# The opening of a decoder block: request order and row sums of the first modulation, and the gates' columns as one transfer

## The chip, the cores and the metric

The kernel runs on one core of a Trainium2 chip. The metric is the device time of one execution in microseconds (us), the median of several runs. Beside it there is one profiled execution, from which every view in this document is taken. Engines are called as the profile calls them: PE is TensorE (matmuls; PEld its weight loads), DVE is VectorE, ACT is ScalarE, POOL is GpSimd, SP is SyncE, whose queue asks for all data transfers (DMA).

## The reference

One layer of a decoder: a modulation, a mixer with three kinds of heads, and a feed-forward part. Only the beginning matters here. For 2048 positions of width 1024:

```python
c_act = jax.nn.silu(c)                                   # 1024 values
mod = c_act @ w_ada[l] + b_ada[l]                        # 1024 x 6144 weights
sh1, sc1, gt1, sh2, sc2, gt2 = [m[:, None, :] for m in jnp.split(mod, 6, axis=-1)]
h = rms_norm(x, g_mix[l]) * (1.0 + sc1) + sh1
y = hybrid_mixer(h, w_in[l], ...)                        # begins with p = h @ w_in
```

The first thing that the mixer does is the projection `h @ w_in` into 3088 columns. It needs `h`, and `h` needs the first two of the six parts of the modulation: `sh1` (columns 0 to 1023 of `w_ada`) and `sc1` (columns 1024 to 2047). The rest of the kernel (attention, mLSTM, gating, output projection, feed-forward) is not touched by the change.

## The kernel before, in words

All of it is one program without loops at run time. Matmuls are made in three passes over split operands (`mm3`, L53 to L56: high x high, high x low, low x high), each operand having been split into a high part (`hh`, `wh`: a rounded copy) and a low part (`hl`, `wl`: what the rounding left).

The opening, in the order of the program text:

- The vector `c` is loaded as rows, turned on PE (`columns`, L382 to L389) and goes through silu on ACT into `cs` (L398), one column for each of eight row pieces of 128.
- Four tiles of x (128 positions each, 512 KB) are loaded and normalised in place (`norm_x`, L513 to L524): squares on ACT (L518), small steps on DVE, a power on POOL (L128), a scaling on DVE (L523).
- `first_mod(0)` (L437 to L447): for the column groups 0 and 2 of `w_ada` (512 columns each: the first half of `sh1` and of `sc1`) eight pieces of 128 rows x 512 columns, 256 KB each, are loaded into tiles `wa` (L410, buffers of the tag hT, of which there are 32). `mod_sum` (L413 to L421) multiplies each piece by its column of `cs` and adds it to an accumulator, all on DVE: one instruction for the first piece (L418), seven more for the others (L420). PE then sums the accumulator over its 128 rows and turns it into four columns, by four matmuls with a column of ones (L441), into a PSUM tile `modp`. With `g_mix` and `b_ada`, loaded as rows and turned by `columns`, DVE makes `sh1` and `a1` for the first four of the eight 128-column pieces of h (L445 to L447).
- The weights of the first column block, `Weights` (L570 to L597): eight pieces `wr` of 128 x 272, loaded by two transfers each, 256 columns of `k_m` and 16 columns of gates (`load`, L585). `cast` makes `wh` on ACT (L595) and `wl` on POOL (L596).
- `first_mod(1)`, the same for the column groups 1 and 3, for the other four pieces of h.
- `make_h(0)` (L555 to L567): for each of the eight pieces k of width, the four tiles of x are turned on PE into a PSUM tile (L560), ACT scales and shifts it into `h32` with columns k of `a1` and `sh1` (L564), DVE copies it into `hh` (L565) and takes the rest into `hl` (L566).
- `head_setup` (L534 to L550): 13 small loads, of which the last is the spatial weights `wsn` (L541); POOL masks them (L543), PE turns them (L549), ACT copies them into `wT` (L550).
- `make_h(1)`: four more tiles of x (L404), normalised, and the same eight pieces.
- The first block of projections (`natural`, L635): eight row tiles, 24 matmuls of 272 columns each, with three PSUM banks, so that three row tiles can be open at once. Then the second block begins (512 columns a matmul).

Small constants stand in the text between and behind these: the identity as bf16 (L97), a selector `selb` (three casts, L821), causal masks `maskb` and `maskT` (L834, L839), all by DVE, from tiles that POOL fills.

What sets the order: outside the hand-ordered stretches the order of each engine's instructions is made by a planner, when the program is built. It takes of the instructions that are ready, by its own estimate of durations, the one that stands first in the program text. From the second to the sixth block of projections of either half of the positions (`manual_schedule`, entered where i is 1 in the loop over `steps`, the last part of the text below) the order of the text holds; behind them it is the planner's again. In both cases each engine carries out its own list strictly in order, and SP's queue asks for transfers in order. A tile with a tag takes one of that tag's buffers and waits until it is free; the tag tmpA, of which the text below takes several small tiles, has two.

Of the kernel before, what the change touches and what calls it, by code (L numbers as in the profile page):

```python
# [8 lines left out]
F32 = mybir.dt.float32  # L9
# [3 lines left out]
ALU = mybir.AluOpType  # L13
# [4 lines left out]
P = 128  # L18
# [7 lines left out]
KT = D // P  # L26
# [3 lines left out]
C_Q, C_K, C_V, C_QM, C_KM, C_VM, C_US, C_G = 0, 512, 1024, 1536, 1792, 2048, 2560, 3072  # L30
# [3 lines left out]
def trunk(  # L34
# [7 lines left out]
    V, A, G, T = nc.vector, nc.scalar, nc.gpsimd, nc.tensor  # L42
    dma = nc.sync.dma_start
    x, out = x[0], out[0]
    w_ada, w_in, w_out, w_up, w_down = w_ada[0], w_in[0], w_out[0], w_up[0], w_down[0]

    def bc(ap, axis, n):
        u = ap.unsqueeze(axis)
        shape = list(u.shape)
        shape[axis] = n  # L50
        return u.broadcast_to(shape)
# [26 lines left out]
    ident = cst.tile([P, P], F32, name="ident")  # L78
# [5 lines left out]
    ones = cst.tile([P, P], F32, name="ones")  # L84
# [9 lines left out]
    cs = cst.tile([P, KT], F32, name="cs")  # L94
    gq8 = cst.tile([P, 1], F32, name="gq8")
    identb = cst.tile([P, P], BF16, name="identb")
    V.tensor_copy(identb, ident)  # L97
    maskb = cst.tile([P, P], BF16, name="maskb")

    class Mem:  # L100
# [24 lines left out]
    pool, pp = Mem(), Mem(PSUM)  # L125
# [246 lines left out]
    def tr_ps():  # L372
        return pp.tile([P, 512], F32, name="trp", tag="trp")
# [4 lines left out]
    def mps():  # L378
        return pp.tile([P, 512], F32, name="mps", tag="mps")


    def columns(dst, n, *src):  # L382
        r = pool.tile([P, P], F32, name="rows", tag="tmpA")
        o = 0
        for v in src:
            k = v.shape[1] // P
            dma(r[o : o + k], v[0].rearrange("(k p) -> k p", p=P))
            o += k
        return transposed(dst, r, n)  # L389
# [12 lines left out]
    def load_x(tt):  # L402
        xt = pool.tile([P, D], F32, name="xt", tag="t4k")
        dma(xt, x[tt * P : (tt + 1) * P, :])  # L404
        return xt

    def load_ada(col, tag):
        for k in range(KT):
            st = pool.tile([P, 512], F32, name="wa", tag=tag)
            dma(st, w_ada[k * P : k * P + P, col : col + 512])  # L410
            yield st

    def mod_sum(tiles):  # L413

        acc = pool.tile([P, 512], F32, name="modacc", tag="t2k")
        for k, st in enumerate(tiles):
            if k == 0:
                V.tensor_scalar(acc, st, cs[:, 0:1], None, op0=ALU.mult)  # L418
            else:
                V.scalar_tensor_tensor(acc, st, cs[:, k : k + 1], acc, op0=ALU.mult, op1=ALU.add)  # L420
        return acc  # L421

    def rest_of_columns():
        r = pool.tile([P, P], F32, name="rows", tag="tmpA")
        dma(r[0:8], g_ffn[0].rearrange("(k p) -> k p", p=P))
        for i, g in enumerate((g_q, g_k)):
            for j in range(2):
                dma(r[8 + i : 9 + i, 64 * j : 64 * j + 64], g)
        dma(r[10:14], b_s[0])
        dma(r[14:16], g_m_out[0].rearrange("(k p) -> k p", p=P))  # L430
        transposed(colA[:, 24:40], r, 16)
        V.tensor_scalar(gq8, colA[:, 32:33], 0.125, None, op0=ALU.mult)


    modp = mps()

    def first_mod(hf):  # L437
        for n in (hf, 2 + hf):
            acc = mod_sum(load_ada(n * 512, "hT"))
            for j in range(4):  # L440
                T.matmul(modp[:, n * 4 + j : n * 4 + j + 1], acc[:, j * P : (j + 1) * P], ones[:, 0:1], start=True, stop=True)  # L441
        if hf == 0:
            columns(colA[:, 0:24], 24, g_mix, b_ada[:, 0:2048])
        sl, o = slice(hf * 4, hf * 4 + 4), hf * 4
        V.tensor_tensor(sh1[:, sl], modp[:, o : o + 4], ba[:, o : o + 4], op=ALU.add)  # L445
        V.tensor_tensor(a1[:, sl], modp[:, 8 + o : 12 + o], ba[:, 8 + o : 12 + o], op=ALU.add)
        V.scalar_tensor_tensor(a1[:, sl], a1[:, sl], 1.0, gm[:, o : o + 4], op0=ALU.add, op1=ALU.mult)  # L447
# [65 lines left out]
    def norm_x(xin):  # L513
        for xt in xin:
            st = pool.tile([P, 2], F32, name="st", tag="st")
            for q in range(2):
                jk = pool.tile([P, 512], F32, name="jk", tag="sq")
                A.activation(jk, xt[:, q * 512 : q * 512 + 512], AF.Square, accum_out=st[:, q : q + 1])  # L518
            V.tensor_tensor(st[:, 0:1], st[:, 0:1], st[:, 1:2], op=ALU.add)
            st = st[:, 0:1]  # L520
            V.tensor_scalar(st, st, 1.0 / D, EPS, op0=ALU.mult, op1=ALU.add)
            rsqrt(st, 1)
            V.tensor_scalar(xt, xt, st, None, op0=ALU.mult)  # L523
        return xin  # L524

    x0 = norm_x([load_x(i) for i in range(4)])
    first_mod(0)


    wT = pool.tile([P, 4, P], F32, name="wT")  # L530
# [22 lines left out]
    hT = {}  # L553

    def make_h(tb, xin=None):  # L555
        xs = xin if tb == 0 else norm_x(xin or [load_x(tb * 4 + i) for i in range(4)])
        for k in range(KT):
            ps = (tr_ps, acc_ps)[k % 2]() if tb == 0 else tr_ps()
            for i in range(4):
                T.transpose(ps[:, i * P : (i + 1) * P], xs[i][:, k * P : (k + 1) * P], ident)  # L560
            h32 = pool.tile([P, TB], F32, name="h32", tag="t2k")
            hh = pool.tile([P, TB], F32R, name="hh", tag="hT")
            hl = pool.tile([P, TB], F32R, name="hl", tag="hT")
            A.activation(h32, ps, AF.Identity, bias=sh1[:, k : k + 1], scale=a1[:, k : k + 1])  # L564
            V.tensor_copy(hh, h32)  # L565
            V.tensor_tensor(hl, h32, hh.bitcast(F32), op=ALU.subtract)  # L566
            hT[tb, k] = (hh, hl)  # L567


    class Weights:  # L570
# [4 lines left out]
            self.width = sum(w for _, w in parts)  # L575
            self.raw, self.tiles = [], []

        def load(self):
            k = len(self.raw)
            if k == KT:  # L580
                return
            raw = pool.tile([P, 512], F32, name="wr", tag=self.tags[k])
            o = 0
            for col, wd in self.parts:
                dma(raw[:, o : o + wd], w_in[k * P : (k + 1) * P, col : col + wd])  # L585
                o += wd
            self.raw.append(raw[:, : self.width])
# [230 lines left out]
    selb = pool.tile([P, 4, P], BF16, name="selb")  # L818
    V.memset(selb, 0.0)
    for r in (32, 64, 96):  # L820
        V.tensor_copy(selb[r : r + 4], bc(ident[r : r + 4, r : r + 4], 2, P))  # L821
    nebs = [pool.tile([P, 512], BF16, name="neb%d" % i, tag="neb") for i in range(2)]
    for t in nebs:
        V.memset(t, 0.0)
# [6 lines left out]
    m32 = pool.tile([P, P], F32, name="m32", tag="tmpA")  # L831
    G.memset(m32, 0.0)
    G.affine_select(m32, m32, pattern=[[-1, P]], compare_op=ALU.is_ge, fill=NEG, base=0, channel_multiplier=1)
    V.tensor_copy(maskb, m32)  # L834
    maskT = pool.tile([P, 4, P], BF16, name="maskT")
    maskf = pool.tile([P, P], F32, name="maskf", tag="tmpA")
    G.memset(maskf, 0.0)
    G.affine_select(maskf, maskf, pattern=[[1, P]], compare_op=ALU.is_ge, fill=NEG, base=0, channel_multiplier=-1)
    V.tensor_copy(maskT, bc(maskf, 1, 4))  # L839
    V.memset(rmask, 1.0)  # L840
    V.memset(rmask.rearrange("p (n l) -> p n l", l=P)[:, :, 0:1], 0.0)

# [82 lines left out]
    def mlstm(qi):  # L925
# [32 lines left out]
        def turned(n):  # L958
# [7 lines left out]
            got["k", n] = kT  # L966

        load(0)
        load(1)
        yield  # L970
# [98 lines left out]
    chores.append(rest_of_mod())  # L1069
    written = ExitStack()  # L1070
    cur = Weights(blocks[0][0], G, ("q2k",) * 3 + ("qhl",) * 3 + ("wr",) * 2)
    for k in range(KT):
        cur.load()
    for k in range(KT):
        cur.cast()
    first_mod(1)
    for n, (half, i) in enumerate(steps):
        if i == 0:
            make_h(half * 2, x0)
            if half == 0:  # L1080
                head_setup()
            make_h(half * 2 + 1)
        elif n == nb - 1:
            x0 = [load_x(8 + t) for t in range(4)]
# [21 lines left out]
        cur = nxt[0]  # L1106
# [51 lines left out]
    hT = {}  # L1158
# [587 lines left out]
```

## Time and profile before

| | us |
|---|---|
| median of 3 runs | 2605.19 |
| lowest, highest | 2605.05, 2606.72 |
| the profiled execution, its own time | 2607.8 |
| span of its profile | 2606.1 |

| engine | busy us | share of the span |
|---|---|---|
| PE | 2530.5 | 97% |
| DVE | 2010.0 | 77% |
| ACT | 1272.8 | 49% |
| POOL | 402.5 | 15% |

How to read the views. A line of the timeline begins with the start in us and the length of a merged run of equal instructions in us; then come engine, line of the kernel, operation, output <- input by the program's names with their shapes, and the count; in brackets, how long the engine was idle before it and what released it. A line of a group has the busy time, the mean duration of one in ns and the idle time before. In a table by windows each engine has its busy time and, in brackets, its number of instructions. The chain of waits goes from instruction to instruction back to whatever released it; its lines are start, length and what it was. Durations of matmuls include a part that overlaps with the next; the pitch from start to start is shorter.

### The profile page before, as it was taken

To read this page: it belongs to the slowest core of one execution; us is meant where nothing else is said; L and a number is where in the kernel's file an instruction comes from. 1 tells how busy PE (TensorE), PEld (TensorE's weight loads), DVE (VectorE), ACT (ScalarE), POOL (GpSimd) and SP (SyncE) were. 2 spreads that over 40 slices of the span, in tenths; PEclk is the share of its full clock that TensorE was granted. 3 is DMA by queue.
4 is the path that set the end of the run, shared out by engine and by line. 5 is a ranking of instruction groups with operands and counts; after the bars stand their busy time and mean duration, and the time that the engine had idled before them with its cause. 6 is when DMAs were issued, how large, how long until landed. Compare 5 with 4: busy or idle time off the path is not lost.

```text
span 2606.1 us, 36311 instructions
## 1 busy us (share of the span) xinstructions
PE 2530.5 (97%) x12521; PEld 2097.9 (81%) x12537; DVE 2010.0 (77%) x3438; ACT 1272.8 (49%) x2424; POOL 402.5 (15%) x532
## 2 busy tenths in 40 slices
PE   5999999999999999999989999999999999999999
PEld 5888888888787877777868888888888888888787
DVE  7657666476388889866589888888888887997797
ACT  4333343432388878844455544454444444444443
POOL 2012310132266556520000000000000000000000
PEclk9999999999999999999999999999999999999999
DMA  7345763454664445266632222255222217658523
GB/s 247 107 120 160 209 209 88 129 152 138 180 164 123 129 126 166 58 195 224 248 89 92 79 89 82 81 201 187 90 81 81 90 65 279 210 176 290 184 93 117
DMA packets 302592, 379.58 MB, mean 146 GB/s; under 512 B 31934, under 2 KB 194588, under 8 KB 300360
## 3 DMA queue, kind: packets, MB, share of 16 engines
q1 hardware_dynamic: 302408, 377.26, 46.1%
q8 instruction: 99, 1.62, 0.3%
q14 instruction: 85, 0.70, 0.1%
HBM read 276.44 MB, written 100.74 MB: 145 GB/s over the span
## 4 chain that ended last, share of the span: by engine, by line
PE 81%; DVE 9%; DMA 4%; ACT 3%; issue 2%; POOL 1%; SPq 0%; DVEq 0%; ACTq 0%; POOLq 0%
PE ub L56 11%; PE ub L54 11%; PE ub L55 11%; PE acc L54 6%; PE acc L56 6%; PE acc L55 6%; PE db L55 4%; PE db L56 4%; PE db L54 4%; PE sp L206 3%; PE tp L259 3%; PE op L245 2%; PE op L246 2%; PE wps L55 2%; PE wps L54 2%
## 5 line engine op out<-in xcount | busy, mean ns | idle before, releaser
L54 PE MATMUL acc<-wh,hh 128*128 128x512 f32 (+2 forms) x768 | 285.5, 373 | 1.9 <-DVE vhl L762 1.2
L54 PE MATMUL ub<-T,wsph 128*128 128x512 f32 x704 | 274.2, 390 | 5.8 <-ACT wsph L1358 5.8
L56 PE MATMUL ub<-T,wspl 128*128 128x512 f32 x704 | 273.7, 389 | 1.6 <-DVE wspl L1359 1.6
L56 PE MATMUL acc<-wh,hl 128*128 128x512 f32 (+2 forms) x768 | 274.2, 360 | 0.3 <-DVE hl L566 0.3
L55 PE MATMUL acc<-wl,hh 128*128 128x512 f32 (+2 forms) x768 | 273.9, 358 | 0.2
L55 PE MATMUL ub<-T,wsph 128*128 128x512 f32 x704 | 273.9, 389 | 0.0
L55 PE MATMUL db<-wspl,wsph 128*128 128x512 f32 x616 | 240.6, 391 | 3.6 <-DVE wspl L1490 3.5
L56 PE MATMUL db<-wsph,wspl 128*128 128x512 f32 x616 | 239.6, 389 | 0.0
L54 PE MATMUL db<-wsph 128*128 128x512 f32 x616 | 238.3, 389 | 0.3 <-ACT wsph L1489 0.3
L1358 ACT CAST wsph<-S 128x512 fp32r<-128x512 f32 x176 | 109.7, 623 | 228.4 <-PE ub L55 162.8
L263 DVE TENSOR_TENSOR plo<-tp,phi 128x512 fp32r<-128x512 f32 (+1 forms) x320 | 187.0, 607 | 31.6 <-ACT phi L262 29.4
L54 PE MATMUL ub<-B,wsph 128*128 128x512 f32 x528 | 207.1, 392 | 2.8 <-ACT wsph L1358 2.8
L56 PE MATMUL ub<-B,wspl 128*128 128x512 f32 x528 | 207.2, 392 | 0.6 <-DVE wspl L1359 0.6
L55 PE MATMUL ub<-B,wsph 128*128 128x512 f32 x528 | 207.0, 392 | 0.0
L223 ACT ACTIVATE L<-L,nm 128x1024 f32<-128x1024 f32 (+2 forms) x192 | 172.6, 903 | 36.0 <-DVE nm L212 34.7
L262 ACT CAST phi<-tp 128x512 fp32r<-128x512 f32 (+1 forms) x320 | 160.0, 521 | 40.2 <-PE tp L259 38.9
L259 PE MATMUL tp<-ident,L 128*128 128x128 f32 x1088 | 177.0, 274 | 2.5 <-POOL L L228 0.6
L206 PE MATMUL sp<-kk,q 128*128 128x512 f32 (+3 forms) x640 | 169.2, 375 | 3.3 <-DVE nm L212 2.2
L1489 ACT CAST wsph<-act 128x512 fp32r<-128x512 f32 x132 | 82.3, 623 | 179.0 <-PE db L55 162.2
L228 POOL TENSOR_SCALAR L<-L,rs 128x1024 f32<-128x1024 f32 (+2 forms) x192 | 167.2, 881 | 11.0
L56 PEld LDWEIGHTS acc<-wh,hl 128*128 128x128 f32 x768 | 145.0, 190 | 22.3 <-DVE hl L566 0.8
L54 PEld LDWEIGHTS acc<-wh,hh 128*128 128x128 f32 x768 | 146.2, 191 | 20.7 <-DVE vhl L762 1.4
(333 smaller groups left out, 5942.9 us busy)
## 6 DMA issues: line engine op xcount, KB each, us to landing
w<-in_w_up_dram SPq DMA_DIRECT2D x88, 512.0 KB
wd<-in_w_down_dram SPq DMA_DIRECT2D x176, 256.0 KB
wa<-in_w_ada_dram SPq DMA_DIRECT2D x96, 256.0 KB
act_d<-yc SPq DMA_DIRECT2D x44, 512.0 KB
act<-act_d SPq DMA_DIRECT2D x44, 512.0 KB
wr<-in_w_in_dram SPq DMA_DIRECT2D x64, 256.0 KB
q<-q_d SPq DMA_DIRECT2D x128, 128.0 KB
hc_d<-hl SPq DMA_DIRECT2D x28, 512.0 KB
```

Source lines behind the costliest of these rows:

```text
L54: T.matmul(ps, lh, rh, start=start, stop=False, skip_group_check=resume)
L55: T.matmul(ps, lh, rl, start=False, stop=False, skip_group_check=resume)
L56: T.matmul(ps, ll, rh, start=False, stop=stop, skip_group_check=resume)
L206: T.matmul(sp[:, b : b + bw], q2[n][:, qs], kk[:, s0 + b : s0 + b + bw], start=n == 0, stop=n == 1 and not last)
L223: A.activation(L[c], L[c], AF.Exp, bias=nm[:, n - 1 : n], scale=-1.0, accum_out=rs[:, c : c + 1])
L228: G.tensor_scalar(t, t, rs[:, 0:1], 1.0, op0=ALU.mult, op1=ALU.mult)
L245: T.matmul(op[:, c0:], vv[:, j, :], hi[:, c0:], start=(j == 0), stop=False)
L259: T.transpose(tp[:, i * P : (i + 1) * P], rows[i][j // 8][:, (j % 8) * P : (j % 8 + 1) * P], ident)
L262: A.copy(hi[:, c0:], tp[:, c0:])
L263: V.tensor_tensor(lo[:, c0:], tp[:, c0:], hi[:, c0:].bitcast(F32), op=ALU.subtract)
L1358: A.copy(hi, src)
L1489: A.copy(hi, v)
```

## The change

It has these parts:

- `first_load` requests all 16 pieces of one half at once. The second half's (`first_load(1)`) stand in the text directly behind `first_mod(0)` and so ahead of the column weights, where they stood behind them.
- In each sum of eight pieces, pieces 0, 2, 4 and 6 stay on DVE. Pieces 1, 3, 5 and 7 are multiplied and summed by PE: four matmuls a piece, with the piece as weights and its column of `cs` as the one moving column, added into the four columns of `modp`. The accumulator's four matmuls add into the same columns. `modp` is set to zero first, and no matmul clears it.
- The 16 gates' columns of all eight pieces of the first column block come in one transfer into a tile `gw` (tag tmpA), and POOL copies them piece by piece into `wr`; the eight transfers of 256 columns stay.
- The copies `hh` of the first row block move from DVE to ACT.
- Six casts of constants (`identb`, three of `selb`, `maskb`, `maskT`) move from DVE to POOL.

```diff
-    V.tensor_copy(identb, ident)
+    G.tensor_copy(identb, ident)
...
     modp = mps()
-
-    def first_mod(hf):
+    V.memset(modp[:, 0:16], 0.0)
+
+    def first_load(hf):
+        return {n: list(load_ada(n * 512, "hT")) for n in (hf, 2 + hf)}
+
+    def first_mod(hf, tiles):
         for n in (hf, 2 + hf):
-            acc = mod_sum(load_ada(n * 512, "hT"))
-            for j in range(4):
-                T.matmul(modp[:, n * 4 + j : n * 4 + j + 1], acc[:, j * P : (j + 1) * P], ones[:, 0:1], start=True, stop=True)
+            acc = pool.tile([P, 512], F32, name="modacc", tag="t2k")
+
+            def add(w, col):
+                for j in range(4):
+                    T.matmul(
+                        modp[:, n * 4 + j : n * 4 + j + 1], w[:, j * P : (j + 1) * P], col,
+                        start=False, stop=True, skip_group_check=True,
+                    )
+
+            for k, st in enumerate(tiles[n]):
+                if k == 0:
+                    V.tensor_scalar(acc, st, cs[:, 0:1], None, op0=ALU.mult)
+                elif k % 2 == 0:
+                    V.scalar_tensor_tensor(acc, st, cs[:, k : k + 1], acc, op0=ALU.mult, op1=ALU.add)
+                else:
+                    add(st, cs[:, k : k + 1])
+            add(acc, ones[:, 0:1])
...
     x0 = norm_x([load_x(i) for i in range(4)])
-    first_mod(0)
+    ada = first_load(0)
+    first_mod(0, ada)
+    ada = first_load(1)
...
-            V.tensor_copy(hh, h32)
+            if tb == 0:
+                A.copy(hh, h32)
+            else:
+                V.tensor_copy(hh, h32)
...
-        def load(self):
+        def load(self, n=2):
...
-            for col, wd in self.parts:
+            for col, wd in self.parts[:n]:
...
-        V.tensor_copy(selb[r : r + 4], bc(ident[r : r + 4, r : r + 4], 2, P))
+        G.tensor_copy(selb[r : r + 4], bc(ident[r : r + 4, r : r + 4], 2, P))
...
-    V.tensor_copy(maskb, m32)
+    G.tensor_copy(maskb, m32)
...
-    V.tensor_copy(maskT, bc(maskf, 1, 4))
+    G.tensor_copy(maskT, bc(maskf, 1, 4))
...
     cur = Weights(blocks[0][0], G, ("q2k",) * 3 + ("qhl",) * 3 + ("wr",) * 2)
+    gw = pool.tile([P, KT, 16], F32, name="gw", tag="tmpA")
+    dma(gw, w_in[:, C_G : C_G + 16].rearrange("(k p) n -> p k n", p=P))
     for k in range(KT):
-        cur.load()
+        cur.load(1)
+        G.tensor_copy(cur.raw[k][:, 256:272], gw[:, k, :])
     for k in range(KT):
         cur.cast()
-    first_mod(1)
+    first_mod(1, ada)
```

More of the change, by code (lines that the diff above doesn't have):

```diff
@@ L411, in load_ada @@
             yield st
[L413 to L421, printed above, removed]
     def rest_of_columns():
```

## The prediction, on record before the result

> **What bounds the kernel now.** I read the page's slices first, then the windows by stage.
>
> ```profile
> span 2606.1 us, 36311 instructions
> PE   5999999999999999999989999999999999999999
> ```
> ```profile
> 0.00:47.28 47.28, 19.09 (x75) 15.73 (x75) 36.70 (x81) 14.55 (x32) 14.60 (x28) 1.00 0.82 275
> 47.28:53.50 6.22, 6.22 (x29) 6.13 (x29) 4.84 (x11) 3.00 (x6) 0.07 (x1) 1.00 0.59 231
> 53.50:78.28 24.78, 24.70 (x194) 23.88 (x193) 17.71 (x43) 16.98 (x40) 2.21 (x4) 1.00 0.42 123
> 78.28:2606.10 2527.82, 2480.47 (x12228) 2052.19 (x12242) 1950.74 (x3305) 1238.23 (x2349) 385.65 (x500) 1.00 0.46 143
> ```
> ```profile
> 78.28 0.39 PE L54 MATMUL acc<-hh,wh 128*128 128x512 f32 x1
> ```
>
> Columns after the window's length: busy us (count) of PE, PEld, DVE, ACT, POOL, then clock, DMA share, GB/s. PE is the bound from 47.28 us on; only ahead of that does it idle, 28 of 47 us. At 78.28 us the second weight block (the first in hand-written order) begins, and PE is busy for 98% of what follows. So a change to the start is worth what it moves 78.28; the rest follows unchanged. The chain of waits says what fills the start:
>
> ```profile
> 2.60 6.42 DMA xt<-in_x_dram
> ...
> 14.44 5.50 DMA wa<-in_w_ada_dram
> ...
> 21.28 2.27 DMA wr<-in_w_in_dram
> ...
> 43.97 1.88 PE mps L441 x8
> ```
> ```profile
> 31.15 5.48 DVE L420 SCALAR_TENSOR_TENSOR modacc<-wa,cs,modacc 128x512 f32<-128x512 f32 x7
> 36.54 0.48 DVE L418 TENSOR_SCALAR modacc<-wa,cs 128x512 f32<-128x512 f32 x1
> 37.06 2.33 DVE L420 SCALAR_TENSOR_TENSOR modacc<-wa,cs,modacc 128x512 f32<-128x512 f32 x3
> 39.30 0.42 DVE L565 CAST hh<-h 128x512 fp32r<-128x512 f32 x1
> ...
> 51.49 0.69 DVE L566 TENSOR_TENSOR hl<-h,hh 128x512 fp32r<-128x512 f32 x1
> ```
>
> Arrivals bound it to 19.9 us (14.44 + 5.50). Then DVE does: the second half's sums run on to 44 us, the first copy of h gets its turn among them at 39.3 only, and the last hl of the first row block is ready at 52.2.
>
> **The change, part by part.**
>
> *Sums.* These groups are of the first 47.28 us (count | busy us, mean ns | idle before).
>
> ```profile
> L420 DVE SCALAR_TENSOR_TENSOR modacc<-wa,cs,modacc 128x512 f32<-128x512 f32 x28 | 21.6, 780 | 0.5
> L441 PE MATMUL mps<-ones,modacc 128*128 128x1 f32 x32 | 7.5, 355 | 16.0 <-DVE modacc L420 16.0
> ```
>
> DVE loses 16 of the 28 additions, 16 x 0.78 = 12.5 us. TensorE gains 16 pieces x 4 = 64 matmuls; eight such took 1.88 us in the chain, so 0.235 each, 15.0 us, inside its 28 idle us. A piece costs TensorE 0.94 us and DVE 0.78; a pair comes every 1.3 us or more (below), so both keep up and arrival becomes the bound. (The Trainium skill, "TensorE: Matmul & The Clock Gate", section "LDWEIGHTS (loading the stationary operand)", gives a weight load as columns over 1.2 GHz, 107 ns for 128: a piece would cost 0.43 us, an estimate from that page, and the last sums would end 1.0 us sooner. The trace's 0.235 us per pair does not agree, and I use the trace.) The memset of the sums' bank lies in the idle start: nothing.
>
> *Order of the requests.*
>
> ```profile
> 14.40:20.00 5.60, 1.33 (x5) 0.93 (x5) 5.34 (x10) 0.00 (x0) 1.05 (x3) 1.00 1.01 354
> 20.00:25.00 5.00, 2.09 (x9) 1.96 (x9) 4.75 (x9) 2.09 (x5) 1.67 (x4) 1.00 0.61 137
> 30.00:35.00 5.00, 0.00 (x0) 0.00 (x0) 4.82 (x7) 1.45 (x2) 0.83 (x2) 1.00 1.02 362
> ```
> ```profile
> wa<-in_w_ada_dram SPq DMA_DIRECT2D x96, 256.0 KB
> ```
>
> The second sixteen pieces, 4.19 MB at 362 GB/s, take 11.6 us behind the first: from 19.9 to about 31. The column weights (eight pieces of 128 x 272 floats, 1.11 MB) come behind them. Between 20 and 25 us such traffic moved 137 GB/s at a share of 0.61, so 225 GB/s when busy: 4.9 us, first piece near 32, last near 36. Before, they were there by 27 and waited; that cover is gone.
>
> *Second sums.* Last piece 31, its four matmuls and the accumulator's four 1.9 us, then 1.1 to the first h that needs them (43.97 + 1.88 to 46.98 in the next rows): 34.0, where it was 47.0. The 32 pieces fill the 32 buffers that h's copies use as well; each is free once its sum has read it, all by 34.
>
> *ACT and POOL.*
>
> ```profile
> L1358 ACT CAST wsph<-S 128x512 fp32r<-128x512 f32 x176 | 109.7, 623 | 228.4 <-PE ub L55 162.8
> ```
> ```profile
> 23.99 6.84 POOL L596 TENSOR_TENSOR wl<-wr,wh 128x272 fp32r<-128x272 f32 x8
> ```
> ```profile
> 46.98 0.78 ACT L564 ACTIVATE h<-trp,sh,a 128x512 f32<-128x512 f32 x1 [5.13 <-DVE a L447]
> 52.98 0.59 ACT L550 COPY wT<-mp 128x512 f32<-128x512 f32 x1 [3.21 <-PE mp L549]
> 53.46 0.64 ACT L518 ACTIVATE jk<-xt 128x512 f32<-128x512 f32 x1
> ```
> ```profile
> 8.90 0.78 POOL L128 TENSOR_TENSOR st<-st,nhalf 128x1 f32<-128x1 f32 x1 [0.92 <-DVE st L521]
> ...
> 14.54 0.20 POOL L832 MEMSET m<- 128x128 f32 x1
> ```
>
> ACT takes 8 copies of h, by L1358 0.62 us each; DVE loses them. From 34.0, four h and copies (0.78 + 0.62) with at most eight weight casts of 0.42 (estimate: L1358 scaled to 272 columns, rounded up) between them last to 43.0; the last hl is ready near 43.7, against 52.2. The casts now wait for the column weights and for POOL's copy of the gates' columns, and h stands behind them on ACT. If the planner puts all eight ahead of every h, the eight pairs (11.2 us) run from 36.4 to 47.6, the last hl comes at 48.3: still 4 us ahead. POOL gets eight copies of the gates' 16 columns, not in this trace: between 0.20 (the memset, larger and without an input) and 0.78 (128x1 with two inputs). I take 0.20, since a copy has one input and no power. With 6.84 / 8 = 0.86 for each wl: 33.5 + 8 x 1.06 = 42; at the upper end 46.6. The gates' tile takes one of two small buffers that the masks use, which POOL, idle then, frees in time. Neither end is later than TensorE needs them, since at the rate of 47.28 to 53.50 (6.22 / 29 = 0.21 us) three row tiles use a piece of nine matmuls in 1.9 us. The other casts moved to POOL (six, none larger than 512 columns, 0.9 us each at wl's rate at most if scaled up to 512) stand in its idle time before 23 us (1.1 busy of 5.6 us in the window from 14.40): nothing; without that cover they would stand ahead of wl, 5 us.
>
> So the first projections start near 34 instead of 47.28.
>
> *The second row block is late next.*
>
> ```profile
> 16.47 8.64 SPq L585 DMA_DIRECT2D wr<-in_w_in_dram  x16
> 25.16 9.75 SPq L410 DMA_DIRECT2D wa<-in_w_ada_dram  x16
> ...
> 41.79 0.38 SPq L541 DMA_DIRECT2D wsn<-in_w_s_dram  x1
> 42.21 2.14 SPq L404 DMA_DIRECT2D xt<-in_x_dram  x4
> ```
> ```profile
> SPq L410 <- DMA wa<-in_w_ada_dram: 5.2, 14, 0.9
> ```
> ```profile
> 3.07 11.70 SPq L410 DMA_DIRECT2D wa<-in_w_ada_dram  x16
> ```
> ```profile
> 45.56 1.79 POOL L543 TENSOR_SCALAR_AFFINE_SELECT wsn<-wsn 128x128 f32<-128x128 f32 x4 [14.73 <-DMA wsn<-in_w_s_dram]
> ```
> ```profile
> 51.89 1.05 PE L549 MATMUL mp<-ident,wsn 128*128 128x128 f32 x4
> ```
> ```profile
> 71.73 0.69 DVE L566 TENSOR_TENSOR hl<-h,hh 128x512 fp32r<-128x512 f32 x1
> ```
>
> SP's queue issues one transfer after another up to x at 42.21, and holds back issues until earlier pieces have landed. The change takes out seven issues (16 to 9) of 8.64 / 16 = 0.54 us: 3.8 us. But the second wa may now go at the pace of the first (11.70 instead of 9.75), 1.9 us back. So wsn and x are asked for 1.9 to 3.8 us earlier; I take 2.9. From wsn hangs ACT's chain: masked on POOL 3.8 us after its issue (42.7, when wl is done), ready 44.5; turned on TensorE, where before it stood 4.5 us in the queue (47.35 to 51.89); then wT, then the squares of x, 1.6 us after the turning. The queue's delay can be anything from 0 to 4.5; I take 2, as TensorE is ahead now: squares at 48.1 instead of 53.46. From there to 78.28 were 24.8 us, of which 5.9 lie behind the last hl (72.4); the work then left is 24 + 9 matmuls at 24.78 / 194 = 0.128, 4.2 us, so 1.6 us can go. Second block at 48.1 + 24.8 - 1.6 = 71.3: **7.0 us earlier**. Ends: all of the 3.8 with no queue delay, with the mask done at 43.7, 68.5 (-9.8); only 1.9 with 4.5, 74.8 (-3.5).
>
> The profiled execution took 2607.8 us, span 2606.1; it would become 2600.8. It lies 2.6 above the median of the runs, 2605.19; from that, 2598.2.
>
> **Rivals.** *First: TensorE alone sets it* (the turning and x's squares are not late). 223 instructions ran from 47.28 to 78.28 and nine projections before: starting at 34, 29 in 6.2 us, 203 at 0.128: 66.2, 12 us earlier, 2593.1. For it: x can come by 48; against: ACT's in-order wait for wT. The windows show 0.21 us per instruction up to 53.50 and 0.128 after, at a granted clock of 1.00 in both. (The same page, section "Part 1: The HAM clock gate (the "warmup" mystery)", says that TensorE runs at half rate until a window of about 3.4 us was busy. By that the sums on TensorE could bring full speed before 34 and save 29 x 0.09 = 2.5 us more of this rival, which is 2590.6. The step in the rows agrees; no row shows whether one-column matmuls count as busy.)
>
> *Second: the lead is lost* at wsn and x: the planner, which orders this stage by its own clock, puts the turning behind all four row tiles, or leaves the column weights' requests where they were. Then x's 1.9 to 3.8 us of SP time is all that is won: 0 to 3.5 us earlier, about 2603.
>
> *Third, slower: the gates' one transfer.* All eight casts now wait for it.
>
> ```profile
> DMA packets 2905, 2.14 MB, mean 203 GB/s; under 512 B 1368, under 2 KB 2416, under 8 KB 2904
> q1 hardware_dynamic: 2904, 2.13, 74.7%
> ```
>
> These are the packets of 16.5 to 27 us: 16 engines x 10.5 us x 0.747 = 125 us of engine time. At 362 GB/s the 488 of 2 KB take 44 and the 1048 of 1 KB 47, so a small one costs 0.025 us. The transfer is 1024 rows of 64 bytes; spread over 16 engines 1.6 us, on one 26 us: asked for near 27.5 it lands at 54, the projections start 8 us later than now, 2613. It decides from where it lands after 45.5, 18 us, fewer than two engines. Against: wsn, also regrouped with partitions outermost, was there 3.8 us after its issue.
>
> **How the numbers follow.** Forecast 0.55, first rival 0.20, second 0.17, third 0.08. A difference of 0.2%, 5.2 us, is about what a measurement of this kernel tells from none. The forecast's own range is 2595.4 to 2601.7, of which some three quarters lie beyond 5.2 us: faster 0.40 + 0.20 = 0.60; within 0.2% 0.15 + 0.17 = 0.32; slower 0.08. The range runs from the first rival's 2593 less 0.5 to the middle of the second and a little beyond, 2592.5 to 2604.
>
> **What would show it.** Right: sums of the second half end near 33 us; casts of wr from 32 us; first projection near 34; SP's x near 39; squares at 45 to 51; the first 128x512 projection of the second block near 71; the stretch behind it 2528 us as before. Wrong: gates' columns landing after 45; wsn's turning still at 50 or later; PE idle over 5 us between the row blocks; a longer stretch after the second block's start.

## The result and the profile after

The change made the kernel slower. The median went from 2606.01 us (2605.05 to 2613.88, 6 runs) to 2622.83 us (2617.54 to 2625.55, 6 runs): ratio 1.0055, 95% interval 1.0041 to 1.0069. The profiled execution after was the quickest of its six, 2617.54 us with a span of 2615.8.

First the windows of the kernel after, cut at its own stages (length; busy us and count of PE, PEld, DVE, ACT, POOL; granted clock, DMA share, GB/s), and the second block's first projection:

```profile
0.00:51.92 51.92, 41.23 (x194) 40.63 (x195) 20.53 (x52) 13.61 (x29) 13.62 (x32) 1.00 0.79 278
51.92:60.00 8.08, 7.11 (x28) 6.17 (x29) 3.17 (x7) 6.76 (x14) 5.74 (x7) 1.00 0.01 3
60.00:68.00 8.00, 8.00 (x64) 7.83 (x64) 1.88 (x10) 3.68 (x11) 1.52 (x5) 1.00 0.34 98
68.00:72.00 4.00, 2.44 (x19) 1.90 (x17) 2.60 (x8) 4.00 (x13) 1.11 (x2) 1.00 0.36 101
72.00:76.00 4.00, 2.11 (x9) 1.48 (x10) 3.17 (x8) 1.90 (x4) 0.55 (x1) 0.68 0.25 70
76.00:80.00 4.00, 4.00 (x20) 4.00 (x20) 3.97 (x9) 2.46 (x5) 0.00 (x0) 0.50 0.55 159
80.00:92.31 12.31, 12.31 (x99) 12.31 (x98) 7.30 (x16) 5.94 (x11) 0.00 (x0) 0.99 0.25 77
92.31:2615.80 2523.49, 2477.14 (x12244) 2050.68 (x12242) 1950.50 (x3305) 1238.01 (x2349) 386.13 (x500) 1.00 0.46 143
```
```profile
92.31 0.40 PE L54 MATMUL acc<-hh,wh 128*128 128x512 f32 x1
```

The second block starts at 92.31 us instead of 78.28, 14.0 later. The span grew by only 9.7, because the stretch behind was 4.3 shorter in this execution; the medians stand 16.8 apart. Runs of one and the same kernel are up to 11 us apart (before: 2601.75 to 2612.68 on the chip of the last four experiments), so the stretch behind, known from one execution of each kernel, explains nothing here, and the start of the second block is the better gauge. For the changed kernel and the twelve experiments below, the change of the median and the change of that start agree within 3 us.

The 14.0 us have two parts. PE's row sums come first (timeline, PE):

```profile
12.20 1.71 PE L437 MATMUL mps<-cs,wa 128*128 128x1 f32 x8
...
32.60 6.99 PE L437 MATMUL mps<-cs,wa 128*128 128x1 f32 x32 [0.54 <-DVE a L454]
39.44 1.85 PE L437 MATMUL mps<-ones,modacc 128*128 128x1 f32 x8
41.40 1.71 PE L437 MATMUL mps<-cs,wa 128*128 128x1 f32 x8
45.13 1.71 PE L437 MATMUL mps<-cs,wa 128*128 128x1 f32 x8
46.94 3.41 PE L437 MATMUL mps<-cs,wa 128*128 128x1 f32 x16
50.22 1.84 PE L437 MATMUL mps<-ones,modacc 128*128 128x1 f32 x8
51.92 0.57 PE L54 MATMUL acc<-wh,hh 128*128 128x272 f32 x1
```
```profile
L437 PE MATMUL mps<-cs,wa 128*128 128x1 f32 x128 | 27.6, 346 | 0.5 <-DVE a L454 0.5
L446 DVE SCALAR_TENSOR_TENSOR modacc<-wa,cs,modacc 128x512 f32<-128x512 f32 x12 | 9.3, 771 | 0.6 <-DMA wa<-in_w_ada_dram 0.3
```

The last two lines are groups of the first 52 us. Four matmuls are written for a piece, and the trace has **eight** records for it: 128 for the 16 pieces, and 128 loads of weights beside them (PEld). An f32 matmul is two loads of weights and two passes here. A piece takes 1.71 us, 16 of them 27.4. The second half's sums end at 52.06 (50.22 + 1.84), where DVE alone ended them at 45.84.

Then the second row block (timeline; ACT, then PE, then DVE, then SP's queue):

```profile
53.10 0.78 ACT L574 ACTIVATE h<-trp,sh,a 128x512 f32<-128x512 f32 x1 [7.48 <-DVE a L455]
...
64.97 0.59 ACT L560 COPY wT<-mp 128x512 f32<-128x512 f32 x1 [1.17 <-PE mp L559]
65.45 0.63 ACT L526 ACTIVATE jk<-xt 128x512 f32<-128x512 f32 x1
```
```profile
64.33 0.60 PE L559 MATMUL mp<-ident,wsn 128*128 128x128 f32 x4
```
```profile
67.83 0.75 DVE L531 TENSOR_SCALAR xt<-xt,st 128x1024 f32<-128x1024 f32 x1 [0.53 <-POOL st L128]
...
72.86 0.75 DVE L531 TENSOR_SCALAR xt<-xt,st 128x1024 f32<-128x1024 f32 x1 [0.66 <-POOL st L128]
```
```profile
26.29 0.38 SPq L1086 DMA_DIRECT2D gw<-in_w_in_dram  x1
26.88 6.29 SPq L598 DMA_DIRECT2D wr<-in_w_in_dram  x8
...
38.21 8.01 SPq L404 DMA_DIRECT2D xt<-in_x_dram  x4
```

x is asked for at 38.21, 4.0 earlier than before, and yet its squares begin at 65.45, 12.0 later: on ACT they stand behind wT, wT waits for the turning on PE at 64.33, and in PE's list some 60 projections of the first block stand ahead of the turning, by its records, where 27 did before. From the squares to the second block it takes 26.9 us instead of 24.8. In this stretch PE runs dry: 2.44 and 2.11 busy of 4 us each between 68 and 76. The granted clock falls to 0.68 and 0.50, and in the four busy microseconds from 76 to 80 there are 20 instructions instead of the 32 of full speed. So 12.0 us are lost ahead of the squares and 2.0 behind them.

### The profile page after: what moved, and what is told of

It is laid out like the page before. It is cut to its first block, busy times and chain, and to the rows that moved or that the text cites. A ratio compares the mean times of both kernels' runs of the same rounds, so it can differ in the third digit from the quotient of the medians.

```text
span 2615.8 us, 36565 instructions
## 1 busy us (share of the span) xinstructions
PE 2554.4 (98%) x12665; PEld 2125.0 (81%) x12665; DVE 1993.1 (76%) x3409; ACT 1276.4 (49%) x2432; POOL 408.7 (16%) x546
## 4 chain that ended last, share of the span: by engine, by line
PE 44%; DVE 5%; DMA 1%; issue 0%; ACT 0%; SPq 0%; DVEq 0%; ACTq 0%
PE ub L56 11%; PE ub L54 10%; PE ub L55 10%; PE db L55 4%; PE db L56 4%; PE db L54 4%; DVE wspl L1506 2%; DMA wd<-in_w_down_dram 1%; PE wps L54 0%; PE wps L56 0%; PE wps L55 0%; DVE T L1201 0%; DVE t2w L1491 0%; DVE t2w L1486 0%; DMA ld<-yt_d 0%
```

## The experiments

Each kernel was measured in three rounds. In the table "sums" is the end of the last accumulator's matmuls, "squares" the first squares of the second row block on ACT, "block 2" the first 128x512 projection, all from each kernel's profile. Ratios are to the kernel before on the same chip, whose medians were 2608.74 (beside e1 to e5), 2608.22 (e6 to e8 and e10) and 2607.34 us (the others).

| kernel | sums | squares | block 2 | median us | ratio (95%) |
|---|---|---|---|---|---|
| before | 45.84 | 53.46 | 78.28 | 2606.01 | |
| after | 52.06 | 65.45 | 92.31 | 2622.83 | 1.0055 (1.0041 to 1.0069) |
| e1 all sums on DVE | 44.07 | 56.72 | 82.54 | 2612.17 | 1.0014 (1.0005 to 1.0024) |
| e2 before, sums on PE | 51.22 | 59.85 | 84.62 | 2616.83 | 1.0029 (1.0018 to 1.0041) |
| e4 order of requests back | 52.56 | 61.19 | 86.20 | 2616.05 | 1.0028 (1.0015 to 1.0040) |
| e5 half of the matmuls | 38.53 | 51.98 | 78.77 | 2606.93 | 0.9994 (0.9984 to 1.0004) |
| e6 head later | 52.16 | 59.34 | 89.33 | 2619.70 | 1.0044 (1.0028 to 1.0061) |
| e7 one piece in eight, head later | 39.77 | 47.18 | 77.17 | 2609.22 | 1.0001 (0.9991 to 1.0010) |
| e8 before, head later | 44.92 | 41.45 | 77.79 | 2610.48 | 1.0010 (1.0001 to 1.0020) |
| e9 half of the matmuls, head later | 38.68 | 45.86 | 75.06 | 2604.41 | 0.9989 (0.9978 to 1.0000) |
| e10 all on DVE, head later | 43.93 | 49.97 | 79.00 | 2608.94 | 1.0003 (0.9993 to 1.0013) |
| e11 e7 with four copies back | 40.37 | 46.21 | 77.12 | 2606.12 | 0.9992 (0.9983 to 1.0001) |
| e12 e11 with two in eight | 40.56 | 45.85 | 77.77 | 2604.43 | 0.9982 (0.9973 to 0.9992) |
| e13 copies back on DVE | 52.15 | 69.11 | 95.42 | 2625.59 | 1.0062 (1.0045 to 1.0079) |

The theory (A): the row sums on TensorE cost nearly twice what the prediction gave them, and all of the start hangs from their end. The rivals: B, the order of the requests; C, the casts and copies that now stand in order on ACT.

**All sums back on DVE (e1).**

```diff
-                elif k % 2 == 0:
+                elif True:
```

> The changed kernel with all eight pieces of each sum on VectorE again; request order, gates' transfer, copies on ScalarE and casts on GpSimd stay changed. Theory A (TensorE's row sums cost twice what was forecast: each f32 matmul is two loads and two matmuls, 1.71 us a piece, 34.8 us in all, and in order they hold up the turning of x and the first projections): the second half's sums end on VectorE near 39 us, the second block starts near 70 to 74 instead of 92, time 2596 to 2602. Rival B (the request order and the gates' transfer make the start late): the second block still starts after 85, time above 2614. Rival C (the eight copies on ScalarE and the work on GpSimd make it late): like B.

Measured: block 2 at 82.54, ratio 1.0014. 9.8 of the 14.0 us come back, so the sums on TensorE are the larger part. But it is still 4.3 later than before, though its sums end 1.8 earlier: A missed (it had the sums end near 39 and block 2 start at 70 to 74), and something else is at work.

**The sums on TensorE alone, in the kernel before (e2).**

```diff
+    V.memset(modp[:, 0:16], 0.0)
...
-            acc = mod_sum(load_ada(n * 512, "hT"))
...
+            for k, st in enumerate(load_ada(n * 512, "hT")):
...
+                elif k % 2 == 0:
+                    V.scalar_tensor_tensor(acc, st, cs[:, k : k + 1], acc, op0=ALU.mult, op1=ALU.add)
+                else:
+                    add(st, cs[:, k : k + 1])
+            add(acc, ones[:, 0:1])
```

> The kernel before with the odd pieces' sums on TensorE and nothing else. Theory A: TensorE has 34.8 us of sums in order, the second half's end near 50 us; second block at 85 to 95, time 2613 to 2624. Rivals B and C: no slower than before, 2600 to 2607.

Measured: 84.62 and 1.0029. The median, 2616.83, lies in A's range, and block 2 0.4 us ahead of its. With the old order of requests, the old copies and the old gates the row sums alone cost 6.3 us of the start.

**The order of the requests back (e4):** the column weights are asked for ahead of the second sixteen pieces again, the rest as changed.

```diff
-    ada = first_load(1)
...
     for k in range(KT):
         cur.cast()
+    ada = first_load(1)
     first_mod(1, ada)
```

> The changed kernel with the second half's sixteen pieces requested behind the column weights again, the rest as changed. Theory A: TensorE's sums still set it, 2614 to 2625. Rival B: back to 2608 or less.

Measured: 86.20 and 1.0028. The median lies in A's range, so the order alone is not the cause, as B had it. But with sums as late as these, it adds 6.1 us. The sums end at 52.56 with the old order and at 52.06 with the new one, so the earlier arrival of the pieces buys 0.5 us, and the column weights behind them come later. With the old order all eight wl were done at 28.07 us and wsn was masked at 42.80, ahead of the end of the sums; with the new one POOL makes six of the wl from 54.26 on and masks wsn behind them, at 59.49. One window from 40 us to the second block, e4 first, then after, shows it in POOL: e4 has 4.6 us of work left there, after 10.5, as the wl come so late.

```profile
40.00:86.20 46.20, 44.36 (x289) 42.72 (x289) 24.18 (x57) 26.15 (x54) 4.58 (x8) 1.00 0.39 123
```
```profile
40.00:92.31 52.31, 47.90 (x288) 45.60 (x288) 24.65 (x57) 29.00 (x62) 10.53 (x17) 0.93 0.34 107
```

PE has the same work in both, 289 and 288 instructions. With the new order it is idle for 4.4 us of the window instead of 1.8, and it is busy 3.5 us longer over that work, at a granted clock of 0.93 instead of 1.00. So the dry stretch between the row blocks and the falling clock come largely with the order of the requests. From before over e2 and e4 to after, the 14.0 us are 6.3 for the sums, 1.6 for the gates' transfer, the copies and the casts together, and 6.1 for the order; taken in another sequence, the shares may differ.

**Half of the matmuls of each odd piece (e5)** takes away half of the suspected cost and leaves the order of the text as it is.

```diff
-            def add(w, col):
-                for j in range(4):
+            def add(w, col, cols=4):
+                for j in range(cols):
...
-                    add(st, cs[:, k : k + 1])
+                    add(st, cs[:, k : k + 1], 2)
```

> The changed kernel with two of the four matmuls of each odd piece left out, so that half of the columns lack the odd pieces: a piece then costs TensorE 0.86 us, what the prediction had reckoned. Theory A: the sums end near 37 us, the second block starts at 70 to 76, time 2596 to 2604. Rivals B and C: within 3 us of the changed kernel.

Measured: the sums end at 38.53, 13.5 earlier; block 2 starts at 78.77, 13.5 earlier. Their end passes through to the second block one for one, so it is shown that the length of the sums sets that start in the changed kernel; B and C, which had allowed 3 us, are out as its only cause. A's own ranges (70 to 76, 2596 to 2604) are missed: at 38.53 the sums end 7.3 us ahead of before, and the second block starts no earlier than before. Its windows show where the lead goes:

```profile
52.00:56.00 4.00, 3.68 (x30) 3.46 (x29) 1.43 (x6) 4.00 (x15) 1.10 (x2) 1.00 0.65 189
56.00:60.00 4.00, 1.73 (x12) 1.17 (x11) 2.56 (x7) 2.61 (x8) 1.10 (x3) 1.00 0.29 95
60.00:64.00 4.00, 3.15 (x14) 2.75 (x15) 3.87 (x9) 2.73 (x4) 0.00 (x0) 0.51 0.46 130
64.00:68.00 4.00, 4.00 (x24) 4.00 (x24) 3.67 (x8) 2.84 (x4) 0.00 (x0) 0.64 0.42 110
```

PE finishes the first row block and has nothing of the second: 3.4 of 12 us are dry, then the clock falls to 0.51 and 0.64. The second theory (D): the second row block's x is late, since the turning of wsn and its wT stand ahead of the squares.

**The head's loads and the turning behind the second row block,** in the changed kernel (e6), in the kernel before (e8), with all sums on DVE (e10), and with one piece in eight on TensorE (e7; `elif k != 7` for `elif k % 2 == 0`):

```diff
             make_h(half * 2, x0)
+            make_h(half * 2 + 1)
             if half == 0:
                 head_setup()
-            make_h(half * 2 + 1)
```

> The changed kernel with the thirteen small loads, the masking, the turning and wT placed behind the second row block's make_h in the text. Theory D (beside A: ScalarE's in-order wT waits for a turning that the planner put behind two row tiles, so that the second row block comes late, TensorE runs dry between the row blocks and its clock falls to half): the squares of x follow the first block's h at once, no dry stretch, no granted clock under 1.00 before the second block; the second block starts at 83 to 87 instead of 92, 2 to 8 us less than the changed kernel, still slower than before because of the sums. Without D: within 2 us of the changed kernel and the clock still falls.

> The kernel before with the small loads behind the second make_h alone. In it TensorE was busy throughout between the row blocks, so D expects little: second block at 76 to 78.5, within 3 us of before.

> All sums on VectorE as in the first experiment, the small loads behind the second make_h. D: the second block starts at 73 to 77 instead of 82.5, the clock stays at 1.00, time 5 to 9 us below the first experiment. Without D: as the first experiment.

> The changed kernel with only the last of eight pieces of each sum on TensorE (four pieces of 32 in all) and the small loads behind the second make_h. A and D together: TensorE's sums 14 us instead of 35, no dry stretch; second block at 68 to 74, time 4 to 9 us below before. If a further cause is at work: second block at 77 or later, no better than before.

Measured: in e6 the squares come 6.1 us earlier and block 2 only 3.0 (89.33). D had 83 to 87 and no falling clock, but PE still runs dry and its clock still falls:

```profile
64.00:68.00 4.00, 2.96 (x23) 2.47 (x21) 2.60 (x8) 1.79 (x7) 1.86 (x4) 1.00 0.57 164
68.00:72.00 4.00, 3.13 (x16) 2.52 (x17) 2.97 (x11) 3.00 (x4) 0.68 (x3) 0.74 0.86 246
```

In e8 the first squares come 12.0 earlier, between the fourth and the fifth h, and block 2 only 0.5, as was expected: in the kernel before, moving the turning wins next to nothing. (PE ran dry there for 1.5 us between 40 and 44, and its granted clock reads 0.54 and 0.60 in the two windows from 44 to 52, so the run does not say what the turning alone is worth.) e10 stands 3.5 us ahead of e1 and its clock does not fall; 5.5 to 9.5 were expected. In e7 the sums end at 39.77 and block 2 starts at 77.17, 1.1 ahead of before, against an expected 4 to 10, which is the reading for a further cause: the lead of 6 us in the sums is lost again between the row blocks. Moving the turning helps with the new order of requests, and is a part of the second cause, not all of it.

The table holds a rival to D, the order of the requests. From the end of the sums to block 2 it takes 32.4 to 33.6 us in the four kernels with the old order (before, e2, e4, e8), although the turning was moved in e8 alone, and 35.1 to 43.3 in all the others. The turning would then be one link of what the late column weights hold up: casts, wl, the mask of wsn, the turning. No kernel has short sums on TensorE and the old order together, so how much of the lead of e5 and e7 the order takes is not shown.

**Both suspected causes taken away (e9):** half of the matmuls, and the head later.

> The changed kernel with two of the four matmuls of each odd row piece left out (so half of the columns of sh1 and a1 lack these pieces) and the head's loads and the turning of wsn behind the second make_h, so that both suspected causes are taken away at once. Theory F, two causes in a row (the length of the row sums on TensorE, then the lateness of the second row block because ACT works its list in order and the turning of wsn stands ahead of the squares of x): squares of x at 46 to 48.5 us instead of 51.98, TensorE is dry for under 2 us between the row blocks instead of 3, second block at 73 to 75.5 instead of 78.77, time 2600 to 2604. Rival G, the second block follows the end of the sums alone (about 40 us behind the first projection at 38.4): second block at 78 to 79, 2605 to 2609.

Measured: block 2 at 75.06, as F expected; the squares, at 45.86, lie 0.1 ahead of its range and the median of 2604.41 0.4 above it. G's ranges are missed. PE loses 1.9 us between the row blocks and the clock stays at 1.00:

```profile
52.00:56.00 4.00, 2.38 (x18) 1.88 (x17) 2.19 (x7) 1.35 (x3) 2.11 (x6) 1.00 0.87 255
56.00:60.00 4.00, 3.75 (x29) 3.01 (x28) 3.97 (x11) 3.79 (x7) 0.00 (x0) 1.00 0.59 175
```

The two edits give 17.3 of the start together, 13.5 and 3.7 more. They show also what there was to win with the odd pieces at half their price and the turning out of the way, in the new order of requests: 3.2 us of the start, a ratio of 0.9989 whose interval touches 1.

**The copies of h.** All eight back on DVE in the changed kernel (e13), and the last four back in e7 (e11: `if tb == 0 and k < 4`).

> The changed kernel with nothing but the eight copies hh of the first row block back on DVE: what this part alone is worth. Theory F: the sums on TensorE still end at 52 and the turning of wsn at 64 still gates the squares of x, so ACT is 5 us freer behind 52 to little use: second block at 89.5 to 92.5 instead of 92.31, 2616 to 2623. Rival: the copies on ACT, in order ahead of casts and squares, are the main loss: second block at 85 to 88, 2610 to 2615.

> The changed kernel with one row piece in eight on TensorE, the head's loads behind the second make_h, and of the eight copies hh of the first row block the last four on DVE again, where they were before. Theory F: ACT, the engine on which h, the copies, the casts and the squares of x stand in order, has 4 x 0.62 = 2.5 us less ahead of the squares: squares at 44.5 to 45.5 instead of 47.18, second block at 74 to 75.5 instead of 77.17, 2604 to 2607 where the kernel without this edit took 2609.2. Rival G: second block at 76.5 to 78, 2607.5 to 2611.

Measured: e13 starts block 2 at 95.42, 3.1 later than after, and both F (89.5 to 92.5) and its rival (85 to 88) are missed, as they are in the median. So the copies on ACT helped the start, and C falls as far as they go; the casts are taken up below. In time the two kernels can't be told apart (1.0062 and 1.0055, with intervals that overlap). In e11 block 2 hardly moved (77.12). The fifth h waits for a1 until 41.95 whoever makes the copies, so the squares come 1.0 earlier and not 2.5, and the last four of them stand on ACT behind a copy of the first results, which waits for PE:

```profile
41.95 0.78 ACT L574 ACTIVATE h<-trp,sh,a 128x512 f32<-128x512 f32 x1 [2.64 <-DVE a L455]
...
48.57 0.20 ACT L526 ACTIVATION_READ_ACCUMULATOR jk<-xt 128x1 f32 x1
50.96 0.37 ACT L674 COPY ev<-acc 128x256 f32<-128x256 f32 x1 [2.19 <-PE acc L56]
51.23 0.63 ACT L526 ACTIVATE jk<-xt 128x512 f32<-128x512 f32 x1
```

By the start of block 2 G was right: the planner put another wait of the same kind in the place of the one removed. The median, 2606.12, lies in F's range and 1.4 below G's.

**Two pieces in eight on TensorE (e12),** else as e11: `elif k % 4 != 3`.

> As the one with four copies back, but two row pieces in eight on TensorE. If DVE's sums set their end there (28 additions of 0.78 us with the first pieces' hl among them), four fewer end them 2 to 3 us earlier, near 38 instead of 40.6, and the second block starts at 72 to 74, 2602 to 2606. If TensorE's pieces of 1.71 us set it, the sums end no earlier or later (40.5 to 43) and the second block starts at 75 to 78, 2607 to 2611.

Measured: the sums end at 40.56, as in e11, block 2 at 77.77. At their end PE's rows follow each other without a gap, so TensorE's price sets it, by the second reading:

```profile
35.33 1.71 PE L437 MATMUL mps<-cs,wa 128*128 128x1 f32 x8
36.90 0.45 PE L570 MATMUL trp<-ident,xt 128*128 128x128 f32 x1
37.14 1.71 PE L437 MATMUL mps<-cs,wa 128*128 128x1 f32 x8
38.71 1.85 PE L437 MATMUL mps<-ones,modacc 128*128 128x1 f32 x8
```

The time, 2604.43, is below that reading's range and lies in the other's. This is the best version: 0.9982 (0.9973 to 0.9992), the only one whose interval lies below 1. But only 0.5 us of its 4.7 (0.18% of 2607.34; the two medians are 2.9 apart) show at the second block; where the rest comes from stays open, and its interval overlaps that of e11.

## Why the prediction was wrong, step by step

**The bound: right.** PE is busy for 98% of what follows the second block's start, and the time went where that start went: 14.0 us later, 16.8 in the medians.

**The sums: the step that failed.** "Eight such took 1.88 us in the chain, so 0.235 each, 15.0 us": the eight were taken for eight written matmuls, and they were the four of one accumulator. The row quoted for it had the means to see this: "L441 ... x32" in the first 47 us, where the program text writes 4 matmuls for each of 4 accumulators, 16. So a piece costs TensorE 1.71 us and not 0.94, the sixteen 27.4 and not 15.0, and "both keep up and arrival becomes the bound" turns round: DVE's part, 0.77 a piece, is done early, and PE falls behind by almost a microsecond a piece. The sums ended at 52.06 instead of about 33, and the first h that needs them came at 53.10 instead of 34.0. What DVE loses was right: 12 additions, 9.3 us, remain of 28.

The step had a second fault: it set the 15.0 us against the 28 idle us of the whole start, and asked only whether a piece keeps up with a piece. In the stretch in which the pieces arrive, PE also has the accumulators' matmuls and the turning of x. In e5, with the odd pieces at 0.85 us, PE was busy for 25.9 of the 26.5 us from 12 to 38.53, 20.6 of them with the sums. So about at the forecast's price, too, TensorE and not arrival sets the end of the sums, 5.5 us later than forecast.

(The Trainium skill's 107 ns a load, which the prediction set against its 0.235, is half of what a record took here, 27.4 / 128 = 0.214, and there are twice as many records as it was applied to. By the section on the clock gate of the same page of the Trainium skill, "TensorE: Matmul & The Clock Gate", a cold TensorE runs at half rate, and that would account for the first factor.) The timeline of e7 agrees: the same group of eight records takes 1.86 us early and 1.03 after PE has turned x.

```profile
27.34 1.86 PE L437 MATMUL mps<-cs,wa 128*128 128x1 f32 x8 [0.54 <-DVE a L454]
...
36.55 0.63 PE L570 MATMUL acc<-ident,xt 128*128 128x128 f32 x2
36.97 1.03 PE L437 MATMUL mps<-cs,wa 128*128 128x1 f32 x8
```

At that pace a piece costs close to the forecast's 0.94; in the changed kernel none of the sixteen ran at it.

**The order of the requests: right in its times, a cost in effect.** x was asked for at 38.21 (forecast 39). The prediction saw that the column weights lose their cover and reckoned that this costs nothing; e4 shows the price once the sums are late, 6.1 us.

**The gates' one transfer: not the cause.** The third rival, the only one on the slower side, is out: it landed by 32.74, where POOL's first copies start.

```profile
32.74 2.81 POOL L1089 COPY wr<-gw 128x16 f32<-128x16 f32 x7 [14.84 <-DMA gw<-in_w_in_dram]
...
54.26 5.27 POOL L609 TENSOR_TENSOR wl<-wr,wh 128x272 fp32r<-128x272 f32 x6 [7.26 <-ACT wh L608]
59.49 1.48 POOL L553 TENSOR_SCALAR_AFFINE_SELECT wsn<-wsn 128x128 f32<-128x128 f32 x4
```

A copy took 0.40 us, between the bounds of 0.20 and 0.78; POOL then waited for ACT, not the other way round. The six casts stood from 7.70 to 17.90 us, ahead of those 14.84 idle us, as forecast; no run took them or the gates' transfer alone.

**ACT: the durations right, the place wrong.** h took 0.78, a copy 0.62, a cast 0.35 (1.06 / 3). But six of the eight casts of the column weights stood behind the fifth h, which waited until 53.10 for a1:

```profile
44.89 0.73 ACT L608 CAST wh<-wr 128x272 fp32r<-128x272 f32 x2
...
53.77 1.04 ACT L608 CAST wh<-wr 128x272 fp32r<-128x272 f32 x3
...
55.24 1.06 ACT L608 CAST wh<-wr 128x272 fp32r<-128x272 f32 x3
```

So the casts waited for the sums too, and wl for the casts until 59.5, and the mask of wsn for the wl. The prediction had that last wait, with the wl done at 42; of the places of the casts it weighed only the case ahead of h.

**The second row block: the right place, the wrong size.** Squares at 48.1 were forecast, and came at 65.45, 17.4 us later, behind sums that ended 19 us later. From there 23.2 us were forecast and 26.9 measured, 3.7 for the dry stretch and the falling clock, which were no term of the sum at all. Together 21.0, which is what lies between 71.3 and 92.31. The second rival named the mechanism, the turning behind all four row tiles (it stood behind some 60 of the 96 projections of the first row block), and priced it at no worse than no change: with TensorE slowed, the same queueing loses time. e5, whose pieces cost TensorE 0.85 us, somewhat less than the forecast's 0.94, shows that a lead of 7.3 us in the sums is lost there all the same: with that price the step behind it would still have failed, and the time would have been that of before (0.9994), not 2598.

**The clock of the first rival.** Its sentence on the rule of the Trainium skill ("TensorE: Matmul & The Clock Gate", Part 1) left open whether one-column matmuls count as busy. The changed kernel speaks against it: PE ran them without a pause from 32.60 to 39.59, still at 6.99 / 32 = 0.218 us a record, and nearly so from 46.94 to 52.06, and the projections behind ran at 7.11 / 28 = 0.254 us up to 60 and at 8.00 / 64 = 0.125 after (second and third row of the windows).

## What to carry to other kernels

Before pricing an instruction from a run of equal records, set the count of records against the count that the program text writes; a factor of two there is worth more than any argument on overlap. Work that is moved to an idle engine comes to lie on the critical path if that engine is the one that starts the next stage and it cannot clear a piece as fast as the pieces arrive. A request that is moved forward pushes back those behind it, and their work can then pile up at the moment when the path needs the engines. And a lead at one stage is worth nothing if the next stage's input stands behind a wait in some engine's ordered list: TensorE then runs dry, and may lose its clock as well.

## What the runs showed of the hardware

- An f32 matmul of 128x128 weights and one column is two pairs of load and pass, 0.214 us each in the changed kernel, 0.43 in all: a row sum of 128x512 costs TensorE 1.71 us there, 1.03 in e7 behind the turning of x, and DVE 0.77.
- The granted clock falls some microseconds after TensorE ran dry: 3.4 dry of 8 us (68 to 76 after) gave 0.68 and then 0.50, and full speed was back only past 80. The dry time alone does not decide it: with 1.9 dry of 8 us it stayed at 1.00 in e9 (52 to 60) and fell in e6 (64 to 72), to 0.74 in the second half of that stretch and 0.83 in the 4 us behind it. In e13, the deepest gap, 1.21 busy of 4 us was followed by 0.52 and 0.63:

```profile
72.00:76.00 4.00, 1.21 (x6) 0.60 (x6) 2.43 (x9) 3.42 (x11) 1.16 (x3) 1.00 0.06 20
76.00:80.00 4.00, 2.11 (x9) 1.61 (x9) 3.34 (x7) 2.12 (x4) 0.49 (x1) 0.52 0.25 72
80.00:84.00 4.00, 4.00 (x24) 4.00 (x23) 3.92 (x8) 2.60 (x5) 0.00 (x0) 0.63 0.48 138
```

- At the start the granted clock reads 1.00 while the same projections take twice their later pitch; the column shows the later fall, not the slow start. In e7, where PE had reached the faster pace at 36.97, the slow stretch from 42 to 46 us does read 0.50.
